# Modulation sums over k: one strided reduction replaced by three additions

## The chip, the cores and the metric

The kernel runs on one core of a Trainium2 chip. A core has TensorE (PE, matmuls), VectorE (DVE), ScalarE (ACT), GpSimd (POOL) and SyncE (SP, which issues the DMAs here), each with its own queue of instructions in a fixed order; they wait for one another through semaphores. SBUF is the memory in which tiles of 128 partitions lie, PSUM takes the matmuls' results. The metric is the time of one execution on the device in microseconds (us).

## The reference

One layer of a decoder trunk: a state-space head group and an attention head group side by side, then a feed-forward part, all steered by six vectors that are computed from a conditioning vector `c`. Only these vectors matter here:

```
c_act = jax.nn.silu(c)                                     # (1, 1024)
mod = jnp.einsum('bd,de->be', c_act, w_ada[l]) + b_ada[l]  # w_ada: 1024 x 6144
sh1, sc1, g1, sh2, sc2, g2 = split(mod, 6)
h = x * (1.0 + sc1) + sh1
y = hybrid_mixer(h, ...)
x = layer_norm(ALPHA * x + (1.0 + g1) * y, ...)
h = x * (1.0 + sc2) + sh2
...
x = layer_norm(ALPHA * x + (1.0 + g2) * ff, ...)
```

`sh1` and `sc1` are needed before anything else can start, the other four much later.

## The kernel before

The 1024 inputs of a matmul are 8 blocks (k) of 128 partitions. `w_ada` comes as 48 tiles, one for each of six sections and eight blocks `j` of 128 outputs; a tile holds 128 partitions x 8 (k) x 128 (outputs), 512 KB in float32. For 44 of the 48, the function `ada_sum` (lines 128 to 135) loads the tile into `raw_ada`, GpSimd multiplies it in place by `c_act` (line 132, one instruction over 1024 elements of each partition), and VectorE adds over k (line 134), which leaves `ada_red`, 128x128. The sum over the 128 partitions that is still missing is a matmul of TensorE with a tile of ones. The other 4 tiles (`j` under `PE_ADA`) go through TensorE alone.

`ada_sum` is called from two places. In the head of the program, `h_tile(j)` makes the 8 blocks of `h`: it takes the sums for sections SC1 and SH1 (12 of them, for `j` = 2 to 7), writes `mod_t` (two small VectorE operations, lines 155 and 157), has ScalarE scale and shift the tile `xt` of the input (line 160), and splits the result into a high and a low part, `h_hl` (line 81 or 83, then a subtraction on VectorE, line 85, with two inputs in SBUF). Every projection is three matmuls with such parts. While the blocks of `h` come, TensorE works on the three projections that take each block as it is ready (`mm_ps` with `dtf_hl`, `b_ps`, `c_ps`). The raw tiles of the head lie in slots that are free then (`ADA_TAGS`: "P", "pt", "cum").

Later, `ada_rest` makes the other 32 sums (SC2, SH2, G2, G1), two at a time, from the state-space part to the middle of the attention part. Their raw tiles lie in the slots "raw", of which there are two, and which the weight tiles `raw_w` of `w_prep` use as well: these are loaded, copied to a high part by GpSimd (line 79) and subtracted by VectorE (line 85).

The order of instructions on each engine comes from a scheduler that plays the program through with its own times and then fixes one order for every queue; the DMAs stand in SP's queue in such an order too. So an edit of one helper can move instructions elsewhere.

Of the kernel before, what the change touches and what calls it, by code (L numbers as in the profile page):

```python
# [12 lines left out]
ALU = mybir.AluOpType  # L13
# [19 lines left out]
def layer_kernel(ctx, tc, x, xT, cols, rows3, w_ada, b_ada, w_in, w_dtf, w_out, ln_rows, w1, w2, out):  # L33
    nc = tc.nc
# [15 lines left out]
    def T4(tag, name, dt=F32, shape=(P, 1024)):  # L50
        return sb.tile(list(shape), dt, name=name, tag=tag, bufs=SLOTS[tag])
# [12 lines left out]
    def load(o, i):  # L64
        return nc.sync.dma_start(out=o, in_=i)
# [62 lines left out]
    def ada_sum(sec, j, tag, name):  # L128

        raw = T4(tag, "raw_ada", shape=(P, KT, P))  # L130
        load(raw, w_ada[sec * 8 + j])
        nc.gpsimd.tensor_tensor(raw, raw, c_act.unsqueeze(2).broadcast_to([P, KT, P]), op=ALU.mult)  # L132
        red = sb.tile([P, P], F32, name="ada_red", tag="q2", bufs=4)
        nc.vector.tensor_reduce(red, raw.rearrange("p k c -> p c k"), axis=mybir.AxisListType.X, op=ALU.add)  # L134
        return red

    hT = []
# [51 lines left out]
    def ada_rest(sec, j):  # L189
        red = ada_sum(sec, j, "raw", "r")  # L190
        yield
        pst = PT("mm", "adar_ps", (P, P))
        if sec in (G1, G2):
            mm(pst, ones, red, True, True)
            if j == 0:
                gsum[sec] = dr.tile([P, 1024], F32, name=f"grow{sec}")
            g = sb.tile([P, P], F32, name="ada_g", tag="q2", bufs=4)
            nc.vector.tensor_copy(g, pst)
            load(gsum[sec][:, j * P:(j + 1) * P], g)
        else:  # L200
            mm(pst[:, 0:1], red, ones[:, 0:1], True, True)
            nc.vector.tensor_tensor(mod_t[:, sec, j:j + 1], pst[:, 0:1], b_t[:, sec * 8 + j:sec * 8 + j + 1], op=ALU.add)
# [1044 lines left out]
```

## Time and profile before

| | us |
|---|---|
| median of 3 runs | 1742.12 (1740.56 to 1743.21) |
| the profiled execution, its own time | 1744.44 |
| its span, first to last instruction | 1742.7 |
| busy in the span: TensorE | 1654.0 (95%) |
| VectorE | 1229.9 (71%) |
| GpSimd | 821.6 (47%) |
| ScalarE | 747.2 (43%) |

The profile is one execution, recorded instruction by instruction. Busy time says how long an engine had something in work, a wait inside an instruction included; a chain of waits says which work the end hung on. The granted clock of TensorE was 0.98 as the mean of the span. The head of the program, in which `h` is made, lasts up to about 65 us, the last of the 44 sums is taken at 703.5 us.

### The profile page before, as it was taken

How to read it: one execution, taken by the hardware profiler on the slowest of the kernel's cores; microseconds unless marked ns; L12 is line 12 of the kernel's file. 1: busy time of each engine (PE TensorE's matmuls, PEld its weight loads, DVE VectorE, ACT ScalarE, POOL GpSimd, SP SyncE). 2: the span in 40 equal slices, each digit the busy share in tenths (PEclk: the TensorE clock that was granted, in tenths of full speed). 3: DMA queues.
4: the chain of work that ended last, by engine and by line, in shares of the span. 5: the costliest groups of instructions: out<-in, count | busy, mean ns of one | idle time of the engine just before them, and what ended most of it. 6: DMA issues, size and time to landing. Idle time of an engine off the chain costs nothing.

```text
span 1742.7 us, 22932 instructions
## 1 busy us (share of the span) xinstructions
PE 1654.0 (95%) x8316; PEld 1368.7 (79%) x8316; DVE 1229.9 (71%) x1898; ACT 747.2 (43%) x1321; POOL 821.6 (47%) x670
## 2 busy tenths in 40 slices
PE   8989899899999999999899999799999999999996
PEld 6777787788877878888778887688888878888885
DVE  7755777686777777676665379986767855646668
ACT  3458355414444444444565334633332334343322
POOL 5121332256566466454442345566656624704535
PEclk9999999999999999999999999899999999999998
DMA  8134343334444534434324644043444596676512
GB/s 331 37 123 147 109 145 109 121 130 151 161 142 170 169 134 167 137 121 132 119 97 130 221 157 169 37 175 133 146 143 160 172 340 212 247 242 205 194 36 96
DMA packets 112032, 268.72 MB, mean 154 GB/s; under 512 B 10128, under 2 KB 37008, under 8 KB 111920
## 3 DMA queue, kind: packets, MB, share of 16 engines
q1 hardware_dynamic: 111920, 267.27, 44.2%
q8 instruction: 65, 1.06, 0.3%
q14 instruction: 47, 0.39, 0.1%
HBM read 194.22 MB, written 64.62 MB: 149 GB/s over the span
## 4 chain that ended last, share of the span: by engine, by line
PE 60%; DVE 15%; DMA 8%; ACT 7%; POOL 5%; issue 4%; SPq 0%; DVEq 0%; ACTq 0%; POOLq 0%
PE mm_ps L62 18%; PE f_ps L957 15%; PE s_ps L1073 9%; PE y_ps L1073 7%; PE s_ps L62 5%; PE o_ps L62 4%; DVE ada_red L134 3%; PE t_ps L546 3%; DMA w_b<-in_w_dram 2%; ACT scores L417 2%; POOL w_b L182 2%; DMA raw_ada<-in_w_ada_dram 1%; DVE w_hl L85 1%; DVE conv_a L346 1%; DVE h_hl L85 1%
## 5 line engine op out<-in xcount | busy, mean ns | idle before, releaser
L62 PE MATMUL mm_ps<-h_hl,w_hl 128*128 128x512 f32 x2016 | 504.5, 400 | 10.9 <-POOL w_hl L79 6.1
L62 PEld LDWEIGHTS mm_ps<-h_hl,w_hl 128*128 128x128 f32 x2016 | 373.5, 191 | 88.3 <-POOL w_hl L79 6.9
L85 DVE TENSOR_TENSOR w_op<-raw_w,w_op 128x512 fp32r<-128x512 f32 (+1 forms) x149 | 186.9, 1260 | 23.2 <-ACT w_op L81 22.6
L957 PE MATMUL f_ps<-h_s,w_op 128*128 128x512 f32 x768 | 183.8, 394 | 6.4 <-ACT h_s L81 3.3
L957 PEld LDWEIGHTS f_ps<-h_s,w_op 128*128 128x128 f32 x768 | 146.0, 190 | 38.4 <-ACT h_s L81 3.7
L524 POOL TENSOR_SCALAR probs<-probs,m 128x128 f32<-128x128 f32 (+7 forms) x128 | 104.5, 822 | 127.3 <-DVE m L523 122.8
L81 ACT CAST w_op<-raw_w 128x512 fp32r<-128x512 f32 (+1 forms) x149 | 114.5, 774 | 100.2 <-PE f_ps L957 53.0
L1073 PE MATMUL s_ps<-w_op,a_op 128*128 128x512 f32 x672 | 153.7, 390 | 1.5 <-DVE a_op L85 1.1
L1073 PEld LDWEIGHTS s_ps<-w_op,a_op 128*128 128x128 f32 x672 | 125.9, 188 | 28.8 <-DVE a_op L85 1.6
L79 POOL TENSOR_SCALAR w_hl<-raw_w 128x512 fp32r<-128x512 f32 x86 | 60.5, 705 | 180.0 <-PE mm_ps L62 126.1
L85 DVE TENSOR_TENSOR a_op<-a_ld,a_op 128x1024 fp32r<-128x1024 f32 x53 | 75.5, 1427 | 98.4 <-ACT a_op L81 98.4
L132 POOL TENSOR_TENSOR raw_ada<-raw_ada,c_act 128x1024 f32<-128x1024 f32 x44 | 88.8, 2027 | 117.1 <-DMA raw_ada<-in_w_ada_dram 99.8
L522 ACT ACTIVATE probs<-probs,m 128x128 f32<-128x128 f32 (+7 forms) x128 | 99.1, 775 | 96.8 <-DVE m L521 86.5
L957 PE MATMUL f_ps<-h_hl,w_op 128*128 128x512 f32 x576 | 136.9, 389 | 0.0
L85 DVE TENSOR_TENSOR w_hl<-raw_w,w_hl 128x512 fp32r<-128x512 f32 x88 | 81.5, 929 | 68.5 <-POOL w_hl L79 68.2
L548 ACT CAST pt_hl<-t_ps 128x512 fp32r<-128x512 f32 (+1 forms) x160 | 84.8, 542 | 100.7 <-PE t_ps L546 97.3
L957 PEld LDWEIGHTS f_ps<-h_hl,w_op 128*128 128x128 f32 x576 | 108.0, 188 | 22.4
L81 ACT CAST a_op<-a_ld 128x1024 fp32r<-128x1024 f32 x53 | 55.7, 1054 | 159.7 <-PE s_ps L1073 80.7
L62 PE MATMUL o_ps<-pt_hl,v_s 128*128 128x256 f32 (+1 forms) x640 | 110.9, 300 | 8.7 <-DVE pt_hl L549 5.4
L549 DVE TENSOR_TENSOR pt_hl<-t_ps,pt_hl 128x512 fp32r<-128x512 f32 (+1 forms) x160 | 99.6, 630 | 23.1 <-ACT pt_hl L548 21.6
L519 DVE CUSTOM_DVE_ANT_0 probs<-s_ps,cumrow 128x128 f32<-128x128 f32 (+7 forms) x128 | 94.8, 750 | 28.9 <-PE s_ps L62 20.1
L1073 PE MATMUL y_ps<-w_op,a_op 128*128 128x512 f32 x504 | 114.7, 389 | 0.0
(254 smaller groups left out, 3136.1 us busy)
## 6 DMA issues: line engine op xcount, KB each, us to landing
raw_w<-in_w_dram SPq DMA_DIRECT2D x57, 512.0 KB, 4.3
a_ld<-ad SPq DMA_DIRECT2D x49, 512.0 KB, 4.4
raw_ada<-in_w_ada_dram SPq DMA_DIRECT2D x48, 512.0 KB, 3.6
raw_w<-in_w_in_dram SPq DMA_DIRECT2D x44, 512.0 KB, 3.7
w_b<-in_w_dram SPq DMA_DIRECT2D x14, 1024.0 KB, 8.0
w2t<-w_b SPq DMA_DIRECT2D x14, 1024.0 KB, 4.3
ad<-a_s SPq DMA_DIRECT2D x28, 512.0 KB, 3.4
raw_w<-w2t SPq DMA_DIRECT2D x28, 512.0 KB, 4.8
```

Of the source, the lines that this page charges most:

```text
L62: nc.tensor.matmul(o, l, r, start=start, stop=stop)
L79: nc.gpsimd.tensor_scalar(hi, raw, 1.0, 1.0, op0=ALU.mult, op1=ALU.mult)
L81: nc.scalar.copy(hi, raw)
L85: eng.tensor_tensor(lo, raw, hi.bitcast(F32), op=ALU.subtract)
L132: nc.gpsimd.tensor_tensor(raw, raw, c_act.unsqueeze(2).broadcast_to([P, KT, P]), op=ALU.mult)
L519: nc.vector.tensor_tensor_reduce(out=pt, in0=sp[:, :W], in1=cum[:, :W], op0=ALU.add, op1=ALU.max, scale=1.0, scalar=-3.0e38, accum_out=m[: ...
L522: nc.scalar.activation(pt, pt, AF.Exp, bias=m[:, 1:2], scale=1.0, accum_out=m[:, 2:3])
L524: nc.gpsimd.tensor_scalar(pt, pt, m[:, 3:4], 1.0, op0=ALU.mult, op1=ALU.mult)
L548: nc.scalar.copy(hl[:, 0, :n], tp[:, :n])
L549: nc.vector.tensor_tensor(hl[:, 1, :n], tp[:, :n], hl[:, 0, :n].bitcast(F32), op=ALU.subtract)
L957: nc.tensor.matmul(o, l, r, start=first and k == 0 and m == 0, stop=last and k == 3 and m == 2, skip_group_check=True)
L1073: nc.tensor.matmul(banks[j], ahl[a_][:, n, js], whl[w_][:, n, :], start=first and d == 0 and n == 0 and m == 0, stop=last and d == ND - 1 ...
```

## The change

The one reduction over k becomes three additions, the first two in place: 4 blocks onto 4 (512 elements of each partition), 2 onto 2 (256), 1 onto 1 (128). Every one of them reads two tensors in SBUF. The lines behind move by two.

```
         red = sb.tile([P, P], F32, name="ada_red", tag="q2", bufs=4)
-        nc.vector.tensor_reduce(red, raw.rearrange("p k c -> p c k"), axis=mybir.AxisListType.X, op=ALU.add)
+        nc.vector.tensor_tensor(raw[:, 0:4], raw[:, 0:4], raw[:, 4:8], op=ALU.add)
+        nc.vector.tensor_tensor(raw[:, 0:2], raw[:, 0:2], raw[:, 2:4], op=ALU.add)
+        nc.vector.tensor_tensor(red, raw[:, 0, :], raw[:, 1, :], op=ALU.add)
         return red
```

VectorE at the head, from the split of block 0 of `h` (`h_hl_130`) to that of block 1 (`h_hl_172`), before:

```order
L85 TENSOR_TENSOR h_hl_130<-xt_127,h_hl_130 128x1024
L134 TENSOR_REDUCE ada_red_179<-raw_ada_176 128x128
L155 SCALAR_TENSOR_TENSOR mod_t_96<-ada_ps_146,col_92 128x1
L157 TENSOR_TENSOR mod_t_96<-ada_ps_146,col_92 128x1
L134 TENSOR_REDUCE ada_red_185<-raw_ada_182 128x128
L398 MEMSET prev_725 128x128
L85 TENSOR_TENSOR h_hl_172<-xt_169,h_hl_172 128x1024
```

And now:

```order
L85 TENSOR_TENSOR h_hl_130<-xt_127,h_hl_130 128x1024
L134 TENSOR_TENSOR raw_ada_176<-raw_ada_176 128x512
L135 TENSOR_TENSOR raw_ada_176<-raw_ada_176 128x256
L136 TENSOR_TENSOR ada_red_179<-raw_ada_176 128x128
L157 SCALAR_TENSOR_TENSOR mod_t_96<-ada_ps_146,col_92 128x1
L159 TENSOR_TENSOR mod_t_96<-ada_ps_146,col_92 128x1
L134 TENSOR_TENSOR raw_ada_184<-raw_ada_184 128x512
L135 TENSOR_TENSOR raw_ada_184<-raw_ada_184 128x256
L136 TENSOR_TENSOR ada_red_187<-raw_ada_184 128x128
L400 MEMSET prev_749 128x128
L85 TENSOR_TENSOR h_hl_172<-xt_169,h_hl_172 128x1024
```

Two reductions stood between the two splits, and six additions stand there now; all else keeps its place.

VectorE a little later, around the split of block 2 (`h_hl_193` before, `h_hl_197` now), before:

```order
L134 TENSOR_REDUCE ada_red_206<-raw_ada_203 128x128
L398 MEMSET prev_985 128x128
L134 TENSOR_REDUCE ada_red_221<-raw_ada_218 128x128
L85 TENSOR_TENSOR h_hl_193<-xt_190,h_hl_193 128x1024
L155 SCALAR_TENSOR_TENSOR mod_t_96<-ada_ps_196,col_92 128x1
L157 TENSOR_TENSOR mod_t_96<-ada_ps_196,col_92 128x1
L134 TENSOR_REDUCE ada_red_227<-raw_ada_224 128x128
```

And now:

```order
L134 TENSOR_TENSOR raw_ada_209<-raw_ada_209 128x512
L136 TENSOR_TENSOR ada_red_204<-raw_ada_201 128x128
L135 TENSOR_TENSOR raw_ada_209<-raw_ada_209 128x256
L400 MEMSET prev_1013 128x128
L136 TENSOR_TENSOR ada_red_212<-raw_ada_209 128x128
L134 TENSOR_TENSOR raw_ada_226<-raw_ada_226 128x512
L157 SCALAR_TENSOR_TENSOR mod_t_96<-ada_ps_200,col_92 128x1
L85 TENSOR_TENSOR h_hl_197<-xt_194,h_hl_197 128x1024
L159 TENSOR_TENSOR mod_t_96<-ada_ps_200,col_92 128x1
L135 TENSOR_TENSOR raw_ada_226<-raw_ada_226 128x256
L134 TENSOR_TENSOR raw_ada_234<-raw_ada_234 128x512
L136 TENSOR_TENSOR ada_red_229<-raw_ada_226 128x128
```

The additions of two or three sums are interleaved, with the split and the two small `mod_t` operations of block 3 between them.

GpSimd's queue in the head is the same before and now: eight products, one L79, two products, one L79, two products. Later, near 180 us, where the third and fourth of the 32 later sums are made, it was before:

```order
L79 TENSOR_SCALAR w_hl_1253<-raw_w_1251 128x512
L132 TENSOR_TENSOR raw_ada_1347<-raw_ada_1347,c_act_94 128x1024
L132 TENSOR_TENSOR raw_ada_1352<-raw_ada_1352,c_act_94 128x1024
L79 TENSOR_SCALAR w_hl_1256<-raw_w_1251 128x512
L79 TENSOR_SCALAR w_hl_1359<-raw_w_1357 128x512
L79 TENSOR_SCALAR w_hl_1362<-raw_w_1357 128x512
```

And now:

```order
L79 TENSOR_SCALAR w_hl_1281<-raw_w_1279 128x512
L132 TENSOR_TENSOR raw_ada_1375<-raw_ada_1375,c_act_94 128x1024
L79 TENSOR_SCALAR w_hl_1284<-raw_w_1279 128x512
L132 TENSOR_TENSOR raw_ada_1382<-raw_ada_1382,c_act_94 128x1024
L79 TENSOR_SCALAR w_hl_1391<-raw_w_1389 128x512
L79 TENSOR_SCALAR w_hl_1394<-raw_w_1389 128x512
```

The second product of the pair stands behind a weight split (L79) that waits for TensorE now, and so does that of the next pair; on SP's queue the second load of this pair moved behind a store.

## Rows read from the trace of the kernel before

**Rows 1.** Busy time by stretch. Columns: the stretch in us from the span's start, its length, then for each engine the busy time (and the count of instructions), the granted share of TensorE's clock, the DMA engines' busy share and GB/s.

```profile
15.00:65.00 50.00, 46.12 (x191) 33.68 (x192) 44.01 (x46) 15.68 (x17) 27.95 (x17) 0.93 0.51 199
65.00:180.00 115.00, 103.81 (x540) 83.62 (x538) 74.31 (x113) 76.57 (x131) 21.17 (x18) 0.97 0.35 114
180.00:460.00 280.00, 262.66 (x1495) 220.69 (x1496) 197.48 (x334) 115.11 (x211) 112.28 (x102) 0.98 0.37 128
460.00:705.00 245.00, 232.10 (x1322) 195.09 (x1321) 190.07 (x415) 109.27 (x242) 146.13 (x153) 0.97 0.47 162
...
sum 1743.00, PE 1653.99 PEld 1368.72 DVE 1229.93 ACT 747.23 POOL 821.64; mean PE 275.67 PEld 228.12 DVE 204.99 ACT 124.54 POOL 136.94
```

**Rows 2.** The chain of work that ended last, its shares by line, of the first 65 us (first row) and of 65 to 705 us (second row).

```profile
by line: DVE ada_red L134 20.6%; DVE h_hl L85 15.3%; PE ada_ps L62 11.1%; PE b_ps L62 9.3%; PE mm_ps L62 8.9%; issue 7.7%; DMA raw_ada<-in_w_ada_dram 6.3%; PE c_ps L62 6.0%; ACT xt L160 3.8%; DVE w_hl L85 3.3%; ACT h_hl L81 3.2%; DVE h_hl L
...
by line: PE mm_ps L62 20.1%; PE o_ps L62 5.8%; issue 5.8%; DMA w_b<-in_w_dram 5.7%; PE s_ps L62 5.3%; DVE ada_red L134 5.1%; ACT scores L417 4.4%; POOL w_b L182 4.4%; PE t_ps L546 3.5%; DVE w_hl L85 3.2%; DMA raw_ada<-in_w_ada_dram 3.1%; DV
```

**Rows 3.** VectorE's groups of instructions, forms kept apart. Columns: line, engine, operation, tiles out<-in, output<-input (partitions x elements, type), count | busy us, mean ns of one | idle us before them.

```profile
L134 DVE TENSOR_REDUCE ada_red<-raw_ada 128x128 f32<-128x1024 f32 x44 | 86.6, 1970 | 18.4 <-POOL raw_ada L132 18.3
...
L788 DVE TENSOR_TENSOR c_acc<-c_acc,res 128x512 f32<-128x512 f32 x4 | 2.6, 681 | 0.0
...
L277 DVE TENSOR_TENSOR wk<-wk 128x256 f32<-128x256 f32 x1 | 0.4, 419 | 0.0
...
L302 DVE TENSOR_TENSOR dte<-tot,cs 128x128 f32<-128x128 f32 x1 | 0.3, 295 | 0.0
```

**Rows 4.** VectorE in order of time, 15 to 59 us. Columns: start us, duration us, engine, line, operation, tiles, shape, count, and in brackets idle time before it.

```profile
15.08 2.74 DVE L85 TENSOR_TENSOR h_hl<-xt,h_hl 128x1024 fp32r<-128x1024 f32 x1 [2.38 <-ACT h_hl L81]
17.74 1.91 DVE L134 TENSOR_REDUCE ada_red<-raw_ada 128x128 f32<-128x1024 f32 x1
...
22.17 2.19 DVE L85 TENSOR_TENSOR h_hl<-xt,h_hl 128x1024 fp32r<-128x1024 f32 x1 [0.23 <-ACT h_hl L81]
24.29 1.95 DVE L134 TENSOR_REDUCE ada_red<-raw_ada 128x128 f32<-128x1024 f32 x1
...
30.14 2.62 DVE L85 TENSOR_TENSOR h_hl<-xt,h_hl 128x1024 fp32r<-128x1024 f32 x1
...
37.26 1.22 DVE L85 TENSOR_TENSOR h_hl<-xt,h_hl 128x1024 fp32r<-128x1024 f32 x1
38.40 2.00 DVE L134 TENSOR_REDUCE ada_red<-raw_ada 128x128 f32<-128x1024 f32 x1
...
57.41 1.23 DVE L85 TENSOR_TENSOR h_hl<-xt,h_hl 128x1024 fp32r<-128x1024 f32 x1
```

**Rows 5.** GpSimd in order of time, 14 to 48 us, the same columns; rows of one kind that follow each other are one row (x8: eight products).

```profile
14.84 16.85 POOL L132 TENSOR_TENSOR raw_ada<-raw_ada,c_act 128x1024 f32<-128x1024 f32 x8 [12.98 <-DMA raw_ada<-in_w_ada_dram]
31.77 1.48 POOL L79 TENSOR_SCALAR w_hl<-raw_w 128x512 fp32r<-128x512 f32 x1
33.22 3.75 POOL L132 TENSOR_TENSOR raw_ada<-raw_ada,c_act 128x1024 f32<-128x1024 f32 x2
41.54 0.62 POOL L79 TENSOR_SCALAR w_hl<-raw_w 128x512 fp32r<-128x512 f32 x1 [4.58 <-PE b_ps L62]
42.13 3.76 POOL L132 TENSOR_TENSOR raw_ada<-raw_ada,c_act 128x1024 f32<-128x1024 f32 x2
```

**Rows 6.** The instructions of line 325, a running sum over 128x16 elements: count, then ns least/median/most, first and last start.

```profile
L325 DVE TENSOR_TENSOR off<-off,tot x6: 152/172/1817, 98.4 to 102.1; 128x16 f32<-128x16 f32 x6
```

**Rows 7.** VectorE in order of time near 1150 us (two-input work of the feed-forward part).

```profile
1159.93 0.68 DVE L965 SCALAR_TENSOR_TENSOR a_c<-a_c 128x512 f32<-128x512 f32 x1
...
1162.84 1.78 DVE L85 TENSOR_TENSOR w_op<-w_s,w_op 128x512 fp32r<-128x512 f32 x1
```

**Rows 8.** GpSimd in order of time, the same stretch.

```profile
1154.10 1.73 POOL L788 TENSOR_TENSOR raw_w<-raw_w 128x512 f32<-128x512 f32 x1
...
1162.32 1.75 POOL L791 TENSOR_TENSOR a_s<-a_c 128x512 f32<-128x512 f32 x1
```

**Rows 9.** GpSimd in order of time, 181 to 214 us.

```profile
183.32 0.62 POOL L79 TENSOR_SCALAR w_hl<-raw_w 128x512 fp32r<-128x512 f32 x1
...
206.06 1.90 POOL L132 TENSOR_TENSOR raw_ada<-raw_ada,c_act 128x1024 f32<-128x1024 f32 x1 [6.33 <-DMA raw_ada<-in_w_ada_dram]
207.93 0.63 POOL L79 TENSOR_SCALAR w_hl<-raw_w 128x512 fp32r<-128x512 f32 x1
213.80 0.62 POOL L79 TENSOR_SCALAR w_hl<-raw_w 128x512 fp32r<-128x512 f32 x1 [5.25 <-DMA raw_w<-in_w_in_dram]
```

**Rows 10.** VectorE in order of time, the reductions that follow those products.

```profile
183.39 1.92 DVE L134 TENSOR_REDUCE ada_red<-raw_ada 128x128 f32<-128x1024 f32 x1 [2.81 <-POOL raw_ada L132]
...
208.00 1.95 DVE L134 TENSOR_REDUCE ada_red<-raw_ada 128x128 f32<-128x1024 f32 x1 [4.08 <-POOL raw_ada L132]
```

**Rows 11.** The chain of work that ended last in order of time, 170 to 310 us. Columns: start us, us, what.

```profile
202.75 3.18 DMA raw_ada<-in_w_ada_dram
...
206.06 1.91 POOL raw_ada L132
208.00 1.96 DVE ada_red L134
209.97 3.68 DMA raw_w<-in_w_in_dram
```

## The prediction

> **What bounds the kernel now.** I read the busy time by stretch first [rows 1]: TensorE is busy 1654 of 1743 us, and the change touches the stretches up to 705 us alone. In 15 to 65 us VectorE is busy 44.0 of 50 us, more than in any other row; from 65 to 705 us TensorE is idle 41.4 of 640 us (11.2 + 17.3 + 12.9) and VectorE has room. Then the chain that ended last, over the first 65 us and over 65 to 705 us [rows 2]: the reductions hold 20.6% of the first (13.4 us, with another 15.3% on the splits `h_hl`), and 5.1% of the second (32.6 us, some 17 of the 32 reductions there at 1.97 us). So the head of the program is bound by VectorE; later the reduction is on the path only now and then, where it gives back a `raw` slot for the next weight load.
>
> **What a reduction and a tree cost alone.** 44 reductions take 1.97 us each [rows 3]. The three additions have rows of their own sizes: 128x512 in SBUF 0.68 us, 128x256 0.42, 128x128 0.29 [rows 3], together 1.39 us: 0.58 us less, if nothing holds them up. Each addition needs the one before it, but dependent two-input operations stand in a row without idle time ahead of them (the 0.0 at the ends of the rows [rows 3]), so I cost that wait at nothing. The Trainium skill ("VectorE: DVE Perf Modes", section "The perf-mode tier table") gives `tensor_reduce` one element a cycle at 0.96 GHz, an estimate of some 1.2 us with a fixed part as an addition's: by it a tree would be dearer by 0.2 us even alone, and the later term below +3 us where I take -5, the whole sum 8 us higher. The row has 1.97 us, and it decides.
>
> **What holds them up.** The tile's split `h_hl`, an operation with two SBUF inputs over 1024 elements, takes 1.22 us when GpSimd is idle (37.26) and 2.74, 2.19 and 2.62 us while GpSimd multiplies (15.08, 22.17, 30.14) [rows 4, 5]. A product had begun at 14.84; it ended 1.87 us later, at 16.7, and the split of 15.08 at 17.8, 1.1 us after that. The small `off` additions show it barest: 0.15 to 0.17 us each, and one of 1.82 us, begun inside a product [rows 6]. Where both engines have such work queued, at 1150 us, they take strict turns: VectorE's 0.68 us operations become 1.78 us, GpSimd's 1.7 [rows 7, 8]. The reductions take 1.82 to 2.04 us right through the products, not more than without [rows 4, 5]: they have one tensor input and take no turn. So the change replaces one operation that doesn't wait for GpSimd by three that each do. The Trainium skill says the same ("SBUF — State Buffer", section "SBUF: two separate sides"): VectorE with two SBUF inputs and GpSimd share a port pair, and the one that comes first keeps it for its whole instruction. The trace agrees (1.82 us for an operation of 0.17).
>
> **Head, 15 to 65 us.** The order of GpSimd's work doesn't change there: products 1 to 8, a weight split (L79), products 9 and 10, an L79 that waits for TensorE's work on tile 3, products 11 and 12. Its loads are there: it runs the first eight without a pause [rows 5], two in a row take 3.75 us, so 1.87 each [rows 5].
> Step 1. When `h_hl` of tile 0 ends at 17.8, product 2 is waiting. VectorE now has three additions, the `mod_t` of tile 1, three additions, `h_hl` of tile 1: seven operations that take turns, against products 2 to 8. Each waits for a product: 7 x 1.87 = 13.1 us, and they cost 2 x 1.39 + 1.22 = 4.0 themselves, less some 0.5 us of overlapping ends: 17.8 + 16.6 = 34.4. Before, that split ended at 24.36 [rows 4]. **Loss 10 us.** All of it is queued ahead of `mod_t` and so of ScalarE's scaling, and TensorE has one tile to work on meanwhile.
> Step 2. Then L79, products 9 and 10 take three more turns (0.6 + 3.7 us), and GpSimd stops at the L79 that waits for tile 3. From there the additions run free: up to the end of `h_hl` of tile 3 that is 4.3 us of turns, 6.2 for trees 3 to 6 and the first addition of tree 7, 2.4 for two splits and 1.2 for smaller work, 14.1 us in all: 48.5. Before, 24.36 to 38.48 [rows 4] was the same 14.1. Five cheaper sums and a split's wait of 1.4 us pay for the turns; the loss stays 10 us.
> Step 3. From tile 3 to tile 7 (before 38.5 to 58.6 [rows 4]) the rest of the trees saves 5.3 x 0.58 = 3.1 us; products 11 and 12 and two L79 cost three or four turns (5 us) where one was paid before (0.85). I take +1 and round with TensorE, which after tile 7 has the same matmuls left: **+10 us for the head**. Bounds: all twelve products waited for in full, less the saving and the waits already paid, 22.4 - 7.0 - 4.0 = +11.4, and more of TensorE's time at the lower of its clocks, 1.2 GHz (0.93 of 2.4 GHz was granted as the mean of 15 to 65 us, with TensorE waiting for tiles [rows 1]), could add 1; on the low side step 1 alone and all later trees free, 10 - 10 x 0.58 = +4. I stay near the upper end since the first eight products are in the queue before the first addition.
> What comes next (the step sizes dt, `cs`, the rows that the state-space part reads) hangs on tile 7, so I pass the 10 us on in full.
>
> **Later, 65 to 705 us.** 17 free trees on the chain at 0.58 us would give -10 us. But where a product ends and GpSimd has something ready, it goes on at once: at 183.32 and 207.93 an L79 of 0.62 us began 0.07 us ahead of the reduction [rows 9, 10]. The first addition then waits 0.6 us and the saving is gone. GpSimd is busy 40% and 60% of the two stretches [rows 1], so an addition that comes at random meets it half the time and waits some 0.4 us: 3 x 0.2 = 0.6 us, a tree's whole saving; yet just after a product GpSimd often waits for the next load (6.3 us ahead of 206.06, 5.2 ahead of 213.80 [rows 9]). I take nine free trees and eight without gain: -5 us, and +3 for GpSimd, which now waits up to 0.68 us for each addition and is on the chain itself. **-2 us.** Bounds: -10 (17 free trees), and +22 (three L79 turns in each of 17: 1.39 + 1.86 - 1.97 = 1.3).
> The scheduler also gives other orders: in the head TensorE takes the third projection of tiles 0 to 2 behind the second of tile 3, the same matmuls later in the queue; near 180 us the second product of a pair moves behind an L79, and its load behind a store on SP's queue. No row prices that; the nearest are single loads of 3.2 to 3.7 us on the chain [rows 11], so -4 to +4, taken at 0. After 705 us nothing is touched.
>
> **Sum.** The profiled execution took 1744.4 us (span 1742.7): + 10 - 2 = 1752.4. It lies 2.3 us above the median of the three runs, 1742.1, so on that footing 1750.
>
> **Rivals.**
> A, the additions don't wait after all (VectorE is let in first, or the pair changes hands inside a product): the head, bound by VectorE, wins 12 x 0.58 = 7 us, later -5: 1742 - 12 = 1730, faster. For it: 1.97 against 1.39 us, 44 times. Against it: every row of 4 to 8. It decides if the first additions at 18 to 34 us take 0.7 us and not 2.5. It would also need the first eight products to be late. Chance 0.12.
> B, no change: the head loses only 4 to 5 us, since TensorE and VectorE catch up once GpSimd stands at its L79 (it was idle 22 of the 50 us [rows 1]), and later trees are mostly free, -5: 1742. For it: the room on GpSimd. Against: the loss comes first, before any tile can be caught up with. Chance 0.20.
> C, turns also later: an instruction of GpSimd is queued at nearly every addition: +10 + 22 = 1774. For it: rows 7 and 8, and GpSimd at 60% from 460 us. Against: its long waits for loads. Decided by the first addition's mean after 180 us: over 1.5 us. Chance 0.08.
> Forecast, a head loss of 7 to 11 and nearly nothing later: 1750, its own range 1746 to 1759. Chance 0.60.
>
> **Numbers.** A measurement of this kernel tells some 0.2% (3.5 us) from no change. Slower by more than that: forecast and C, 0.68. Within it: B, 0.20. Faster: A, 0.12. For 8 in 10 the range leaves out C and the further part of A, and reaches from 1735 (late gains at their bound, a small head loss) to 1761 (head +12, late +4, order +3).
>
> **What would show it.** In the profile after: the three additions' mean far over 0.68, 0.42 and 0.29 us in the first 60 us; products of GpSimd with gaps or 2.5 us long from 20 to 40 us; the second `h_hl` ending near 34 us, the fourth near 48, the eighth near 69; TensorE's idle time in 15 to 65 us up by some 8 us; the trees after 180 us between 1.4 and 2.0 us in sum. Wrong if the second `h_hl` ends before 28 us, or if the same matmul as before stands over 5 us elsewhere by 180 us than at 75 us: then the head was made up, or the order decides.

## The result, and the profile after

The changed kernel takes 1766.54 us (median of 4 runs, 1765.49 to 1767.52), the kernel before 1741.71 us beside it (4 runs, 1740.56 to 1743.21): ratio 1.0144, 95% interval 1.0129 to 1.0159, 24.8 us slower. The direction was forecast, the size was not: 1750 and at most 1761 stood there.

Busy time by stretch in the changed kernel, the counterpart of [rows 1] (columns as there; the stretches are set some 10 us later, since the work is):

```profile
15.00:75.00 60.00, 49.27 (x195) 34.18 (x196) 51.23 (x70) 16.18 (x18) 30.00 (x17) 0.86 0.43 166
75.00:190.00 115.00, 103.17 (x538) 82.48 (x536) 72.81 (x117) 76.05 (x129) 21.80 (x19) 0.99 0.34 111
190.00:475.00 285.00, 262.47 (x1488) 219.94 (x1489) 191.57 (x366) 116.82 (x208) 109.53 (x101) 0.98 0.38 127
475.00:725.00 250.00, 234.60 (x1309) 196.25 (x1308) 193.06 (x441) 108.20 (x244) 153.36 (x154) 0.95 0.47 159
```

In the first stretch VectorE is busy 51.2 of 60 us, TensorE idle 10.7 us where it was idle 3.9 [rows 1]. VectorE in order of time there, changed kernel, the counterpart of [rows 4] (L134 to L136 are now the three additions):

```profile
15.18 2.75 DVE L85 TENSOR_TENSOR h_hl<-xt,h_hl 128x1024 fp32r<-128x1024 f32 x1 [2.38 <-ACT h_hl L81]
17.85 2.38 DVE L134 TENSOR_TENSOR raw_ada<-raw_ada 128x512 f32<-128x512 f32 x1
20.26 2.00 DVE L135 TENSOR_TENSOR raw_ada<-raw_ada 128x256 f32<-128x256 f32 x1
22.30 1.87 DVE L136 TENSOR_TENSOR ada_red<-raw_ada 128x128 f32<-128x128 f32 x1
...
24.22 2.25 DVE L134 TENSOR_TENSOR raw_ada<-raw_ada 128x512 f32<-128x512 f32 x1
26.50 2.00 DVE L135 TENSOR_TENSOR raw_ada<-raw_ada 128x256 f32<-128x256 f32 x1
28.54 1.87 DVE L136 TENSOR_TENSOR ada_red<-raw_ada 128x128 f32<-128x128 f32 x1
30.58 2.66 DVE L85 TENSOR_TENSOR h_hl<-xt,h_hl 128x1024 fp32r<-128x1024 f32 x1
...
46.12 1.21 DVE L85 TENSOR_TENSOR h_hl<-xt,h_hl 128x1024 fp32r<-128x1024 f32 x1
...
68.04 1.23 DVE L85 TENSOR_TENSOR h_hl<-xt,h_hl 128x1024 fp32r<-128x1024 f32 x1
```

And GpSimd, the counterpart of [rows 5]:

```profile
14.95 17.21 POOL L132 TENSOR_TENSOR raw_ada<-raw_ada,c_act 128x1024 f32<-128x1024 f32 x8 [13.09 <-DMA raw_ada<-in_w_ada_dram]
...
33.69 4.36 POOL L132 TENSOR_TENSOR raw_ada<-raw_ada,c_act 128x1024 f32<-128x1024 f32 x2
```

An addition of 128x128, 0.29 us alone [rows 3], takes 1.87 us, which is the length of a product: each addition waits for one. The second split `h_hl` ends at 33.2 us (before 24.4), the fourth at 47.3 (38.5), the eighth at 69.3 (58.6 [rows 4]). GpSimd's first eight products take 17.21 us in place of 16.85 [rows 5]: over the same turns it loses 0.4 us.

From there on the distance grows once more. The matmuls of the last 16 sums (line, engine, operation, tiles, count: ns least/median/most, first and last start), in the kernel before and in the changed one:

```profile
L62 PE MATMUL adar_ps<-ada_red,ones x32: 271/275/447, 459.9 to 734.3; 128*128 128x128 f32 x32
```

```profile
L62 PE MATMUL adar_ps<-ada_red,ones x32: 270/275/421, 473.3 to 754.9; 128*128 128x128 f32 x32
```

The first stands 13.4 us later, the last 20.6; the end of the span 22.5 (1765.2 and 1742.7). So 10.6 us come from the head, 10.0 from what lies between the eighth split and the last of the sums, and 1.9 from behind it; the medians are 24.8 us apart, which leaves 14 for the last two together. Between the end of the eighth `h_hl` and that last matmul TensorE's busy time is nearly the same (1.2 us more), its idle time is not. Stretch, length, busy time by engine, clock, DMA as in [rows 1], before and after:

```profile
58.64:734.30 675.66, 634.22 (x3552) 528.79 (x3552) 483.47 (x911) 315.87 (x612) 291.57 (x287) 0.97 0.40 137
```

```profile
69.27:754.90 685.63, 635.46 (x3529) 527.57 (x3528) 476.45 (x965) 316.06 (x610) 296.71 (x287) 0.97 0.40 134
```

TensorE waits 50.2 us in place of 41.4, although VectorE is busy 7 us less. Over the whole span waits are not all of the loss: the same 8316 matmuls keep TensorE busy 1662.2 us, 8.2 more than before, at a mean granted clock of 0.975 in place of 0.980. All four runs of the changed kernel lie at 0.971 to 0.975, those of the kernel before at 0.977 to 0.985. The stretch of the last 16 sums shows it, before and after (its granted clock is the third number from the end, 0.98 and 0.96 of 2.4 GHz):

```profile
459.90:734.30 274.40, 261.50 (x1494) 220.14 (x1493) 209.97 (x464) 123.06 (x272) 157.45 (x166) 0.98 0.46 158
```

```profile
473.30:754.90 281.60, 265.79 (x1493) 222.85 (x1492) 211.81 (x490) 121.78 (x271) 164.29 (x167) 0.96 0.45 152
```

The additions of the 32 later sums in the changed kernel (VectorE's groups, 75 to 760 us, columns as in [rows 3]):

```profile
L134 DVE TENSOR_TENSOR raw_ada<-raw_ada 128x512 f32<-128x512 f32 x32 | 29.7, 929 | 26.2 <-POOL raw_ada L132 26.1
...
L135 DVE TENSOR_TENSOR raw_ada<-raw_ada 128x256 f32<-128x256 f32 x32 | 15.7, 492 | 0.3
...
L136 DVE TENSOR_TENSOR ada_red<-raw_ada 128x128 f32<-128x128 f32 x32 | 11.4, 355 | 0.8 <-DMA grow<-ada_g 0.6
```

Together 1.78 us for a sum (929 + 492 + 355 ns), still less than the reduction's 1.97. A tree that is shorter than what it replaces, on an engine that is busy less, and 10 to 14 us lost behind the head: this is what the experiments are about.

### The profile page after: what moved, and what is told of

Same layout as the page of the kernel before. It is cut to its first block, busy times and chain, and to the rows that moved or that the text cites. A ratio compares the mean times of both kernels' runs of the same rounds, so it can differ in the third digit from the quotient of the medians.

```text
span 1765.2 us, 23017 instructions
## 1 busy us (share of the span) xinstructions
PE 1662.2 (94%) x8316; PEld 1372.4 (78%) x8316; DVE 1235.6 (70%) x1986; ACT 749.1 (42%) x1323; POOL 829.7 (47%) x670
## 4 chain that ended last, share of the span: by engine, by line
PE 59%; DVE 16%; ACT 8%; POOL 6%; DMA 6%; issue 4%; SPq 0%; DVEq 0%; ACTq 0%; POOLq 0%
PE mm_ps L62 17%; PE f_ps L959 15%; PE s_ps L1075 9%; PE y_ps L1075 6%; PE s_ps L62 4%; PE o_ps L62 3%; POOL w_b L184 3%; PE t_ps L548 2%; ACT scores L419 2%; DVE raw_ada L134 2%; DVE w_hl L85 1%; DMA w_b<-in_w_dram 1%; DMA y_raw<-yd 1%; DMA raw_ada<-in_w_ada_dram 1%; DVE raw_ada L135 1%
## 5 line engine op out<-in xcount | busy, mean ns | idle before, releaser
L79 POOL TENSOR_SCALAR w_hl<-raw_w 128x512 fp32r<-128x512 f32 x86 | 61.5, 718 | 196.2 <-PE mm_ps L62 116.1
L85 DVE TENSOR_TENSOR a_op<-a_ld,a_op 128x1024 fp32r<-128x1024 f32 x53 | 79.6, 1504 | 95.0 <-ACT a_op L81 95.0
L62 PE MATMUL o_ps<-pt_hl,v_s 128*128 128x256 f32 (+1 forms) x640 | 117.1, 304 | 8.4 <-DVE pt_hl L551 5.1
```

Of the source, the lines that this page charges most:

```text
L62: nc.tensor.matmul(o, l, r, start=start, stop=stop)
L79: nc.gpsimd.tensor_scalar(hi, raw, 1.0, 1.0, op0=ALU.mult, op1=ALU.mult)
L85: eng.tensor_tensor(lo, raw, hi.bitcast(F32), op=ALU.subtract)
```

## The experiments

Times are medians; differences are to the kernel before, run beside them on the same chip (1741.1 to 1741.8 us in the four groups).

### Which sums lose: head, later, first half, last half

The tree in some sums only, the reduction in the rest. The condition shown picks the head; `tag == "raw"` picks the later sums, and with `sec in (SC2, SH2)` or `sec in (G2, G1)` beside it their first or last 16:

```diff
-        nc.vector.tensor_reduce(red, raw.rearrange("p k c -> p c k"), axis=mybir.AxisListType.X, op=ALU.add)
+        if tag != "raw":
+            nc.vector.tensor_tensor(raw[:, 0:4], raw[:, 0:4], raw[:, 4:8], op=ALU.add)
...
+        else:
+            nc.vector.tensor_reduce(red, raw.rearrange("p k c -> p c k"), axis=mybir.AxisListType.X, op=ALU.add)
```

The head alone. 

> The three additions in the 12 sums of the head alone; the 32 later sums keep the reduction. Theory T (turns with GpSimd cause the head's loss): the last additions of the first trees again end with a product, the second h_hl split ends near 33 us, and all that follows comes 9.4 us late, as in the changed kernel at 75 us: 1741.7 + 9.4 = 1751. Rival O (a good part of the changed kernel's 25 us comes from the order that the scheduler makes of the rest): the rest has nearly the order of before here, so 1751 too, but the delay at 75 us and that at the end agree within 2 us. If the end is over 4 us away from the delay at 75 us, order decides even with one-input sums.

Measured: 1753.67 us, +12.1, ratio 1.0065 (1.0045 to 1.0084). The eighth split ends at 68.2 us, 9.5 later than before, so T's delay is there. In the one execution that was profiled, the fastest of four (1748.16 us), the end is only 3.7 us later, which is rival O's mark (over 4 us apart); by the medians (12.1 against 9.5) it isn't. That execution had a granted clock of 0.981, the other three 0.977, so it doesn't decide.

The later sums alone. 

> The three additions in the 32 later sums alone; the head keeps the reduction. Expected by difference: 25 - 9.4 = +15 us, 1757, with nothing lost at 75 us. Theory T (turns also later) and rival O (order) and rival S (the raw slot is held from the first addition to the last, 6.1 us on average where the reduction took 2.0) all give this sum; they differ in where it is lost: S between 180 and 370 us, where the three additions are 2 to 7 instructions apart; T wherever GpSimd is busiest, 460 to 705 us; O anywhere, also after 725 us, where no sum is made. If it is 1742 to 1747, head and later losses don't add and need each other.

Measured: 1758.12 us, +16.6, ratio 1.0096 (1.0080 to 1.0113). Head and later part add up to 28.7 us, a little more than the change as a whole. The later part isn't free even with an undisturbed head: in its trace the eighth split ends at 58.8 us (58.6 before), the first matmul of the last 16 sums stands 4.1 us later than before and the last 12.3.

The first 16 of the later sums. 

> The tree in the first 16 of the 32 later sums alone (the scale and shift of the second norm, added up between about 180 and 460 us); the 12 sums of the head and the last 16 keep the one reduction. The tree in all 32 cost 16 us. Three theories of that loss. T, turns with GpSimd: it is spread over both halves, with more in the second, where GpSimd has more to do (40% busy before 460 us, 60% after): about +6 us here, 1748. S, the three additions stand apart in VectorE's queue and hold the weight slot longer, which delays the next weight load: in the trace of the changed kernel the slots are held longer only between 180 and 370 us, so all of the loss is here: 1754 to 1758. O, the scheduler's order gives a loss of its own that is not tied to the place: no number, but then the two halves need not add up to 16.

Measured: 1746.45 us, +5.4, ratio 1.0020 (1.0008 to 1.0032).

The last 16. 

> The tree in the last 16 of the later sums alone (the two gate rows, 460 to 705 us and the last ones a little later). T, turns: about +9 us, 1751. S, slots held longer: nothing, 1740 to 1744, since the additions that end these trees wait for a slot of their result just as the one reduction did. O: anything within some +-5 us of 1742, not the rest of the 16 us.

Measured: 1754.53 us, +13.4, ratio 1.0073 (1.0058 to 1.0088). S, the weight slot held longer, falls: it had all of the loss in the first half. T is near in both. O had no number for the first half and at most 5 us for the second, which is passed; the two halves add up to 18.8 us, all 32 to 16.6.

### Is it the order of the work?

A change of three instructions moves others in every queue. A placebo: the reduction cut in two, which moves work about but takes no turns with GpSimd.

```diff
-        nc.vector.tensor_reduce(red, raw.rearrange("p k c -> p c k"), axis=mybir.AxisListType.X, op=ALU.add)
+        for h in range(2):
+            cs_ = slice(h * 64, h * 64 + 64)
+            nc.vector.tensor_reduce(red[:, cs_], raw.rearrange("p k c -> p c k")[:, cs_], axis=mybir.AxisListType.X, op=ALU.add)
```

> No additions: each reduction is cut into two over 64 columns each, so the same strided work in two instructions with one input each, no turns, some 0.1 us more for each sum. It moves the scheduler's order as the change did, without turns. T: +1 us in the head at most, 1743, and the same times as before later. O: the end moves by 5 us or more either way from 1742, with the delay growing in steps between 180 and 900 us.

Measured: 1742.02 us, +0.5, ratio 1.0002 (0.9988 to 1.0016). This order costs nothing; that says nothing of others.

Then turns without a tree. Behind each later reduction three tiny operations of 128x1:

```diff
         nc.vector.tensor_reduce(red, raw.rearrange("p k c -> p c k"), axis=mybir.AxisListType.X, op=ALU.add)
+        if tag == "raw":
+            for _ in range(3):
+                nc.vector.tensor_tensor(red[:, 0:1], red[:, 0:1], red[:, 0:1], op=ALU.max)
```

In the twin the last line is

```diff
+                nc.vector.tensor_reduce(red[:, 0:1], red[:, 0:1], axis=mybir.AxisListType.X, op=ALU.max)
```

> The one reduction stays in all sums; behind each of the 32 later ones VectorE gets three tiny operations in a chain, 128x1 elements, each a maximum of one column of the sum with itself: two inputs in SBUF, so it takes turns with GpSimd, at 0.15 us of its own. The values don't change. Read against its twin below, which has the same number of operations in nearly the same places. T, turns: each waits for a GpSimd operation about as an addition of the tree does: over 10 us slower than the twin. S and O: within 4 us of the twin, since both have the same chain, and neither holds a weight slot longer than the kernel before.

> The twin: the three tiny operations behind each later sum are reductions of one column to itself, with one input in SBUF, so they take no turn. The values don't change. All theories: 3 x 0.15 us x 32 = 14 us more work for VectorE, which has room there, so 1742 to 1748; T adds that the kernel with two-input operations is over 10 us slower than this, S and O that the two are alike.

Measured: 1741.62 us with two inputs (ratio 1.0002, 0.9986 to 1.0017), 1738.52 with one (0.9983, 0.9972 to 0.9993): 3.1 us apart, not the 10 that T expected, and with intervals that just overlap. The 96 operations, with two inputs and with one:

```profile
L137 DVE TENSOR_TENSOR ada_red<-ada_red 128x1 f32<-128x1 f32 x96 | 20.7, 226 | 1.1
```

```profile
L137 DVE TENSOR_REDUCE ada_red<-ada_red 128x1 f32<-128x1 f32 x96 | 13.2, 149 | 1.1
```

With two inputs they wait 7.5 us in all, and less than half of it reaches the end. The twin gives VectorE 13 us more to do and is still 2.6 us faster than the kernel before, by an interval that leaves out 1: a changed order can gain as well as lose.

A larger dose on the last 16 sums, and its one-input twin (`tensor_reduce(red, red.unsqueeze(2), ...)` in the last line):

```diff
+        if sec in (G2, G1):
+            for _ in range(4):
+                nc.vector.tensor_tensor(red, red, red, op=ALU.max)
```

> The one reduction stays in all sums; behind each of the last 16 come four chained two-input operations of 128x128 on the sum (its maximum with itself), 0.29 us each alone, 1.16 us in all, so that VectorE holds GpSimd up about as long as a tree does (1.39 us), while the weight slot is released by the reduction and the first operation stands where it did. Values don't change. T in the sense that GpSimd is held up or VectorE waits: +8 to +13 us over the twin with one-input operations. Q, or T only through the weight slot that a waiting tree holds: within 4 us of the twin.

> The twin of the kernel with four two-input operations: four one-input operations of 128x128 (a reduction over an axis of length one) behind each of the last 16 sums. Values don't change, all other engines' orders are the same. Both theories: 16 x 1.1 us more work on VectorE, which has room, 1740 to 1748.

Measured: 1752.35 us with two inputs (ratio 1.0055, 1.0040 to 1.0070) and 1751.02 with one (1.0052, 1.0037 to 1.0067). The turns are worth 1.3 us, no difference that can be told; but the twin without any turn is 9.2 us slower than the kernel before, where "both theories" had at most +6. So an order of the work, or 18 us more of VectorE's time (16 x 4 operations of 0.28 us) in that part, can lose 9 us by itself.

### The same order with and without turns

These runs left two things in the tree mixed: where its instructions stand, and that they take turns. To part them, each addition becomes an operation of the same output size with one input, a reduction over an axis of length one:

```diff
-        nc.vector.tensor_tensor(raw[:, 0:4], raw[:, 0:4], raw[:, 4:8], op=ALU.add)
-        nc.vector.tensor_tensor(raw[:, 0:2], raw[:, 0:2], raw[:, 2:4], op=ALU.add)
-        nc.vector.tensor_tensor(red, raw[:, 0, :], raw[:, 1, :], op=ALU.add)
+        nc.vector.tensor_reduce(raw[:, 0:4], raw[:, 0:4].unsqueeze(3), axis=mybir.AxisListType.X, op=ALU.add)
+        nc.vector.tensor_reduce(raw[:, 0:2], raw[:, 0:2].unsqueeze(3), axis=mybir.AxisListType.X, op=ALU.add)
+        nc.vector.tensor_reduce(red, raw[:, 0, :].unsqueeze(2), axis=mybir.AxisListType.X, op=ALU.add)
```

First for the kernel with trees in the last 16 sums (+13.4). 

> Compared with the kernel that has the tree in the last 16 sums alone (1754.5, 13 us over the kernel before). Each of its three additions there becomes an operation of the same output size with one input: a reduction of 512, 256 and 128 columns over an axis of length one, so the values are only passed on and these 16 sums leave seven of their eight parts out. Every engine's order is the same in both, and the weight slot is held by the same three operations; only the turns with GpSimd are gone. An operation takes about as long as the addition alone (an estimate: 0.65, 0.4 and 0.25 us, from the reduction of 1024 contiguous elements in 1.21 us). T, turns: nearly all of the 13 us goes, 1741 to 1745. Q, the places in VectorE's queue (the three stand up to 39 operations apart, and the first stands so early that VectorE waits for GpSimd's product in front of its queue, 11.1 us in 8 waits): nearly all of it stays, 1751 to 1755.

Measured: 1752.02 us, +10.2, ratio 1.0055 (1.0040 to 1.0070). Here Q held: in that kernel's order most of the loss is there without any turn. Waits of TensorE from 460 to 740 us (engine, line, for whom: us in total, times, longest), in the kernel before and in this one:

```profile
PE s_ps L62 <- DVE m L519: 1.8, 3, 0.7
```

```profile
PE s_ps L62 <- DVE m L524: 7.8, 7, 2.4
```

The row maxima `m` of the attention part come later, and the matmuls of the next scores wait for them. Which instruction stands ahead of them, I didn't settle.

Then for the changed kernel itself, all 44 sums. 

> The same with all 44 sums, head included, against the changed kernel (1766.5): the three additions as one-input operations of the same output sizes that pass values on, so the sums leave seven of eight parts out; the orders of TensorE, ScalarE, GpSimd and SyncE are the same in both kernels, VectorE's too but for two weight splits that swap places with an operation of a sum. T: the head gains (12 sums at 0.6 us less, no turns: -5 to -7) and nothing is lost later, 1733 to 1740. Q: the head gains as much, the later 13 to 15 us stay, 1748 to 1754.

Measured: 1744.53 us, +2.7, ratio 1.0010 (0.9995 to 1.0025). Every engine's order is in fact the same in both kernels, VectorE's without exception. The time lies between the two ranges, since the head's gain that both had in them didn't come. What decides is the part behind the head: from the eighth split to the matmul of the last sum it takes 668.1 us, where the changed kernel takes 685.6 and the kernel before 675.7.

```profile
59.66:727.80 668.14, 628.89 (x3532) 522.80 (x3531) 461.99 (x965) 316.40 (x610) 289.80 (x287) 0.98 0.41 138
```

So in the changed kernel's own order it is T: **22.0 of its 24.8 us are turns** and what follows from them. The weight slots are held from the same first to the same last operation here, and nothing is lost behind the head, so S falls for the changed kernel too. What is left, new order and shorter operations taken together, is 2.7 us, which can't be told from nothing; no run has the one reduction in this order, so the two aren't parted and may cancel. The 32 later sums here (75 to 760 us):

```profile
L134 DVE TENSOR_REDUCE raw_ada<-raw_ada 128x512 f32<-128x512 f32 x32 | 21.7, 680 | 30.1 <-POOL raw_ada L132 30.1
...
L135 DVE TENSOR_REDUCE raw_ada<-raw_ada 128x256 f32<-128x256 f32 x32 | 13.2, 413 | 0.3
...
L136 DVE TENSOR_REDUCE ada_red<-raw_ada 128x128 f32<-128x128 f32 x32 | 8.9, 277 | 0.3
```

1.37 us a sum, in place of 1.78: the additions of the changed kernel wait 13.0 us (56.8 less 43.8). VectorE's idle time ahead of the first operation, 30.1 us for products that aren't done, is no less here than there (26.2): that wait at the front of the queue isn't what the 22 us are.

Last, the turns switched on in parts (the same four conditions, the head's shown), the order still the same on every engine:

```diff
+        if tag != "raw":
+            nc.vector.tensor_tensor(raw[:, 0:4], raw[:, 0:4], raw[:, 4:8], op=ALU.add)
...
+        else:
+            nc.vector.tensor_reduce(raw[:, 0:4], raw[:, 0:4].unsqueeze(3), axis=mybir.AxisListType.X, op=ALU.add)
...
```

> All five engines keep the order of the changed kernel, instruction by instruction. The 12 sums of the head are the tree's real additions; in the 32 later sums each addition is an operation of the same output size with one input, which takes no turn and passes values on, so those sums leave seven of eight parts out. With the changed kernel at 1766.5 and the one with one-input operations everywhere at 1744.5, the turns of all 44 sums are worth 22 us in this order. Theory T: the head's turns are the first 9 to 10 us (TensorE's matmuls stand 9 us later at 75 us in the one than in the other), so 1753 to 1755 here. Rival R, head turns that are made up later, so that the later ones carry more: under 1750.

> The other way round, in the same order: one-input operations in the 12 sums of the head (seven of eight parts left out there), real additions in the 32 later ones. T: 1744.5 + 12 to 13 = 1757: each later addition waits for what GpSimd has begun (13.0 us in 96 additions, by their durations in the two profiles) and holds GpSimd up by 7 us, and nearly all of it reaches TensorE. R, or a later price that only exists behind a late head: under 1752, or over 1760 if the head's turns are free.

> Same order again; real additions in the first 16 later sums alone (up to about 460 us), one-input operations that leave parts out in the head and in the last 16. In the profiles of the changed kernel and of the one without turns, TensorE's distance grew by 8 to 9 us from 75 to 450 us. T: 1744.5 + 6 to 9 = 1750 to 1753. If the turns cost something in the attention part only, 1743 to 1746.

> Same order; real additions in the last 16 sums alone (from about 460 us), the rest one-input operations that leave parts out. T: 1744.5 + 5 to 9 = 1749 to 1753, and the two halves together about what all 32 cost. In another order of the work (tree in the last 16 alone against its one-input twin) the same 16 trees' turns cost only 2.5 us: if that holds in every order, 1746 to 1748 here.

| turns in | median us (ratio, 95%) | over no turns (1744.5) | the additions' wait, us |
|---|---|---|---|
| the head | 1756.75 (1.0082, 1.0068 to 1.0096) | 12.2 | |
| all 32 later sums | 1757.80 (1.0092, 1.0076 to 1.0107) | 13.3 | 13.4 |
| the first 16 of them | 1750.54 (1.0056, 1.0035 to 1.0077) | 6.0 | 7.6 |
| the last 16 | 1750.21 (1.0051, 1.0037 to 1.0065) | 5.7 | 6.7 |
| all 44 | 1766.54 (1.0144, 1.0129 to 1.0159) | 22.0 | |

(The kernel before took 1741.77, 1741.79 and 1741.71 us beside the first four, the one without turns and the last, so that they can be set side by side.)

The wait in the last column is the additions' time less that of the one-input operations: for all later sums, from these groups of VectorE (65 to 760 us), 30.2 + 15.5 + 11.5 less 43.8:

```profile
L135 DVE TENSOR_TENSOR raw_ada<-raw_ada 128x512 f32<-128x512 f32 x32 | 30.2, 945 | 27.9 <-POOL raw_ada L132 27.9
...
L136 DVE TENSOR_TENSOR raw_ada<-raw_ada 128x256 f32<-128x256 f32 x32 | 15.5, 483 | 0.3
L137 DVE TENSOR_TENSOR ada_red<-raw_ada 128x128 f32<-128x128 f32 x32 | 11.5, 358 | 0.7 <-DMA grow<-ada_g 0.5
```

The four came out as T had them (within 2 us of the head's range, at the number for all later sums, inside the ranges of both halves). Head and later part add up to 25.5 us, all together to 22.0, the halves to 11.7 against 13.3: nearly additive. Every microsecond that a later addition waits costs the kernel some 0.8 to 1.0 us. Not all of that is TensorE waiting. Busy time over the whole span, in the kernel without turns, the one with all later turns and the changed kernel:

```profile
PE 1652.0 (95%) x8316; PEld 1366.9 (79%) x8316; DVE 1210.0 (70%) x1986; ACT 749.0 (43%) x1323; POOL 822.5 (47%) x670
```

```profile
PE 1656.5 (94%) x8316; PEld 1369.6 (78%) x8316; DVE 1221.5 (70%) x1986; ACT 748.8 (43%) x1323; POOL 826.8 (47%) x670
```

```profile
PE 1662.2 (94%) x8316; PEld 1372.4 (78%) x8316; DVE 1235.6 (70%) x1986; ACT 749.1 (42%) x1323; POOL 829.7 (47%) x670
```

Their spans are 1739.3, 1754.6 and 1765.2 us, their mean granted clocks 0.981, 0.978 and 0.975. So 4.5 of 15.3 us with the later turns, and 10.2 of 25.9 with all of them, are the same matmuls at a lower clock (busy time times clock is 1620 to 1621 us in all three), and the rest is idle time of TensorE. No run holds the clock fixed, so what the turns would cost without that stays open.

### Shortening the sum without turns

The weights of each tile laid out with k innermost, so that one reduction reads contiguous elements:

```diff
-        nc.gpsimd.tensor_tensor(raw, raw, c_act.unsqueeze(2).broadcast_to([P, KT, P]), op=ALU.mult)
-        nc.vector.tensor_reduce(red, raw.rearrange("p k c -> p c k"), axis=mybir.AxisListType.X, op=ALU.add)
+        rv = raw.rearrange("p a b -> p (a b)").rearrange("p (c k) -> p c k", k=KT)
+        nc.gpsimd.tensor_tensor(rv, rv, c_act.unsqueeze(1).broadcast_to([P, P, KT]), op=ALU.mult)
+        nc.vector.tensor_reduce(red, rv, axis=mybir.AxisListType.X, op=ALU.add)
```

(and the tiles transposed to match where `w_ada` is laid out, but for the four whose sums TensorE makes)

> The reduction stays, but w_ada's tiles are laid out with k innermost, so that the 8 numbers it adds lie side by side. If its 1.97 us come from the stride of 512 bytes between them, it now takes 1.2 us, takes no turns, and the head, bound by VectorE, gains 12 x 0.7 = 8 us: 1734, a version faster than both. If the reduction is slow whatever the layout, 1742. If GpSimd's product gets slower with c_act in the inner position, the head is bound by GpSimd instead: over 1742.

Measured: 1734.72 us, -6.8, ratio 0.9958 (0.9942 to 0.9974), faster than both kernels. Its reduction and GpSimd's product:

```profile
L135 DVE TENSOR_REDUCE ada_red<-raw_ada x44: 1195/1210/1222, 18.3 to 694.1; 128x128 f32<-128x1024 f32 x44
```

```profile
L133 POOL TENSOR_TENSOR raw_ada<-raw_ada,c_act x44: 2344/2398/3437, 14.9 to 683.5; 128x1024 f32<-128x1024 f32 x44
```

The product in the kernel before:

```profile
L132 POOL TENSOR_TENSOR raw_ada<-raw_ada,c_act x44: 1891/1899/2926, 14.8 to 690.4; 128x1024 f32<-128x1024 f32 x44
```

The reduction takes 1.21 us in place of 1.97, at the price of a product of 2.40 us on GpSimd in place of 1.90 (medians). It is the shortest sum for VectorE here, shorter than the three additions even when they don't wait (1.37), and it takes no turn.

The forecast time came, 1734, but not for its reason. GpSimd's first eight products and the eighth split in this kernel:

```profile
14.92 22.68 POOL L133 TENSOR_TENSOR raw_ada<-raw_ada,c_act 128x1024 f32<-128x1024 f32 x8 [13.06 <-DMA raw_ada<-in_w_ada_dram]
```

```profile
59.77 1.23 DVE L85 TENSOR_TENSOR h_hl<-xt,h_hl 128x1024 fp32r<-128x1024 f32 x1
```

The head wins nothing: the eighth split ends 2.4 us later than before (61.0 us), and GpSimd's products take 22.68 us for 16.85 [rows 5]. The gain lies in the last 16 sums, from their first matmul to their last:

```profile
460.10:725.40 265.30, 254.51 (x1487) 213.01 (x1486) 196.44 (x455) 120.96 (x267) 169.45 (x166) 1.00 0.48 162
```

That is 9.1 us less than before, and 7.0 of it is TensorE's busy time, at a granted clock of 1.00 where it was 0.98. Over the whole span TensorE's idle time is the same in both profiled executions (88.3 and 88.7 us). So the number was luck, and whether the shorter reduction or the order that came with it brought the gain isn't shown.

## Why the forecast was too low

**Head, steps 1 to 3: right.** +10 us was forecast for TensorE after tile 7; the eighth split ends 10.6 us later, the second at 33.2 us (34.4 forecast), the fourth at 47.3 (48.5), TensorE's idle time is up 6.9 us (8). The seven turns of step 1 are there one by one. The lower clock, which the forecast had in its upper bound alone (+1 us), came too: 0.86 was granted in 15 to 75 us, where 15 to 65 us had 0.93 [rows 1]; its share of the head isn't known. Switched on alone in the changed kernel's order, the head's turns are worth 12.2 us.

**What the shorter sums give back: wrong in the head and later.** Step 2 paid for turns with "cheaper sums", rival A gave 12 x 0.58 = 7 us in the head, and the later term counted -5 us for nine free trees. With all 44 sums at 1.37 us and no turns the kernel is no faster (+2.7 by the medians; in its profiled execution, the fastest of ten, the span ends 3.4 us earlier than before, 1739.3 against 1742.7). In the head, the shares of the chain over the first 75 us in that kernel, and under them VectorE's fourth, fifth and eighth split there and the busy time from 15 to 65 us:

```profile
by line: PE mm_ps L62 23.7%; PE ada_ps L62 20.5%; PE b_ps L62 15.3%; PE c_ps L62 15.2%; DVE h_hl L85 6.2%; DMA raw_ada<-in_w_ada_dram 5.5%; DVE an L291 1.9%; issue 1.8%; ACT L350 1.7%; ACT xt L162 1.7%; ACT L289 1.5%; ACT conv_a L350 1.1%; 
```

```profile
35.99 2.13 DVE L85 TENSOR_TENSOR h_hl<-xt,h_hl 128x1024 fp32r<-128x1024 f32 x1
...
45.39 2.58 DVE L85 TENSOR_TENSOR h_hl<-xt,h_hl 128x1024 fp32r<-128x1024 f32 x1
...
58.43 1.23 DVE L85 TENSOR_TENSOR h_hl<-xt,h_hl 128x1024 fp32r<-128x1024 f32 x1
```

```profile
15.00:65.00 50.00, 45.52 (x188) 33.29 (x188) 40.25 (x70) 15.19 (x16) 27.98 (x16) 0.93 0.51 198
```

The sums are all but gone from the chain, which was theirs to 20.6% of its first 65 us [rows 2], and TensorE has it; the eighth split ends at 59.7 us, 1.0 us later than before. "The head is bound by VectorE" was too simple. VectorE is busy only 3.8 us less (40.25 for 44.01 [rows 1]), in part because the fourth and fifth split, 1.22 and 1.21 us before, now meet products and wait. And TensorE stands right behind it, busier than VectorE in that very row (46.1 of 50 us [rows 1]). So in this order time taken off VectorE in the head bought nothing, while the turns put it 9.6 us behind (eighth split at 69.3 and 59.7 us).

**Later, -2 us: the step that failed.** The mechanism was named (additions that wait for what GpSimd has begun, and GpSimd for them), and its check held: the trees after 180 us were to take 1.4 to 2.0 us in sum, they take 1.78 (measured from 75 us on; an addition waits no more than forecast, 0.41 us a tree where 0.6 stood). What was wrong is what I set those waits against. I took them off the 0.58 us that a tree saves ("a tree's whole saving"), called the rest no gain, and did so for the 17 trees of the chain alone. In the runs the saving, with the new order, is worth nothing that can be measured, and the waits of all 32 trees count nearly in full: the later turns alone cost 13.3 us by the medians, where the additions wait 13.0 to 13.4 us. Against the forecast's terms: the -5 for free trees and the 0 for the order came out at +2.7 together, the head's saving included, and the eight trees "without gain" and the +3 for GpSimd at +13. Why the one counts and not the other was not shown by a run of its own. One reading, untested: a reduction's length is known when the work is put in order, and other work can be put there to fill it, while a wait for GpSimd comes unforeseen, ahead of whatever stands next in VectorE's fixed order.

**The order, -4 to +4, taken at 0.** In the changed kernel order and shorter operations together are +2.7 us, and neither is known alone. The bounds were too narrow as such: other kernels of this study lost 9 to 10 us with no turns at all, by their order or by VectorE's work in the attention part. In other orders than the changed kernel's the turns cost less: 2.5 us for trees in the last 16 sums (1752.02 against 1754.53; 5.7 in the changed kernel's order), and 1.3 and 3.1 us in the runs with operations behind the reduction. So the price near 1 us for each us of waiting holds for the changed kernel's order, and why it is less elsewhere stays open.

**After 705 us nothing is touched: nearly right.** The last sum's matmul stands 20.6 us later, the end 22.5.

**The rivals.** A fell in the first addition (2.38 us, 0.7 wanted). B fell in the head, which wasn't made up. C came nearest in its sum (1774), but not by its mark: the first addition's mean was to be over 1.5 us and is 0.93 from 75 us on. Of its 22 us for the later turns 13 were there all the same, by shorter waits of all the trees.

**Turns and the distance of the elements.** The Trainium skill ("SBUF — State Buffer", section "SBUF: two separate sides") has VectorE with two SBUF inputs and GpSimd share a port pair; the pairs of kernels in one order show it at its cleanest, 0.93 us for an addition and 0.68 for a one-input operation with the same output. By the Trainium skill ("VectorE: DVE Perf Modes", section "The perf-mode tier table") a reduction was some 1.2 us, an estimate, where the row had 1.97. The runs have both: 1.21 us over contiguous elements, 1.97 over elements 512 bytes apart.

## What to carry to other kernels

An instruction that is shorter alone can cost more in its place: before VectorE's one-input operation is replaced by two-input ones, look at what GpSimd has queued beside each, and count each wait at up to its full price. Count the saving at nothing while another engine is as busy, even where the chain of waits runs through the work that gets shorter: here the chain named the reductions for 20.6% of the head, and TensorE was right behind. To learn whether a loss comes from what instructions do or from where they stand, build a twin that has the same instructions in the same places without the one property in question. And look where a gain arises before you believe its reason: the kernel with k innermost met its forecast time without any gain in the place that the forecast had for it.

## What the runs showed of the hardware

- A reduction over an axis of length one takes as long as an addition of the same size that doesn't wait: 680, 413 and 277 ns for 512, 256 and 128 columns, beside 681, 419 and 295 [rows 3].
- A reduction of 1024 elements takes 1.21 us when they are contiguous and 1.97 us at 512 bytes' distance; the product on GpSimd goes the other way, 2.34 us at the least and 2.40 in the median with c_act's eight factors innermost, 1.89 and 1.90 with them outermost, so the half microsecond is not waiting.
